# Attention logits from three products instead of four, in a decoder layer on one core

## The chip, the core and the metric

The kernel runs on one NeuronCore of a Trainium2 chip. TensorE multiplies matrices into PSUM (the program uses eight banks of 128 x 512 float32), VectorE and ScalarE work on SBUF and PSUM, GpSimd and SyncE mostly issue transfers. The metric is the device time of one execution in microseconds; lower is better. The kernel before took 1721.38 us, the median of three runs (1719.90 to 1727.16).

## The reference: what is computed

One decoder layer over 1024 tokens of width 1024 in float32: a recurrent branch (RWKV-7, 8 heads of 64) and an attention branch run side by side, are merged by gates, and a SwiGLU feed-forward follows. The change is in the attention branch. An indexer picks at most 256 keys for each query; here that choice is already a bias, 0 for a chosen key and a large negative number for the others. What is left, per head and block of 128 queries:

```python
qb, k, v = rope(q)[block], rope(k), v              # heads of 64
logits = einsum('bqhd,bqkhd->bqhk', qb, kg).astype(float32) * Dh ** -0.5
logits = where(valid, logits, -inf)
prob = softmax(logits, axis=-1)
out = einsum('bqhk,bqkhd->bqhd', prob, vg)
```

## The kernel before, in words

Products that need float32 accuracy are made from two reduced-precision parts of each operand, hi = x rounded and lo = x - hi. The dense layers add three products, hi x hi, hi x lo and lo x hi (`mm3`: line 142 and line 143 alternate over the contraction, line 147 follows). The attention logits of a head contract over only 64 numbers, so hi and lo of the query are stacked to 128 rows, and the key's part stands in both halves: the first product gives (q_hi + q_lo) k_hi, the second (q_hi + q_lo) k_lo. That is two products of 128 rows for each head and each piece of up to 512 keys (line 1081).

The 1024 tokens are worked in two halves of 512. `attend(half)` goes over 4 pairs of heads and, in each, over 4 blocks of 128 queries: 16 units. Block b looks at (b + 1) x 128 keys, 128 to 512 in the first half (one piece) and 640 to 1024 in the second (two pieces). A unit has these steps:

- logits (line 1081) into PSUM tiles called `mix`; line 1083 on VectorE adds the bias, moves the tile to SBUF as `L` and keeps the running maximum; line 1086 on ScalarE takes the exponential and its sum;
- turn (line 1095): TensorE transposes the exponentials in 128 x 128 tiles, ScalarE copies them to SBUF as `pt` (line 1097);
- values (line 1105): transposed probabilities times values, in plain float32, 64 columns a head, so that the two heads of a pair write the two halves of PSUM's rows; the sums of a pair of heads stay in one `mix` bank for four units;
- close: the sums of the exponentials are inverted and multiplied in.

The steps are staggered: with the logits of unit i go the transposes of unit i - 1 and the values of unit i - 2. There are five `mix` banks, shared with the recurrent branch, and three `acc` banks for the dense layers.

TensorE's order is the order in which the code is written. Dense work is a generator in a list named `fill`; `pump(n)` takes steps from it worth n products. In the first half the attention itself is in that list, two of its steps for two steps of the gate products (`blend`), and the recurrent branch (`rwkv`, with the 64-row products of line 573, the row sums of line 603 and the transposes of line 720) pumps the list. In the second half `attend` is the outer loop: each `yield n` pumps n products of the feed-forward layer of the first half. The other engines' order is set by a scheduler when the program is built.

Keys, queries and values come from DRAM, where `proj_qk` has put them (`rope_b` stores each rotated tile on SyncE's queue, line 352). `load` and `load_q` bring those of the next pair of heads on GpSimd's queue two units ahead. Weights arrive on SyncE's queue, or on ScalarE's in part of the program, in three staging buffers (`wst`), and lines 116 and 117 split them into hi (ScalarE) and lo (VectorE).

## Time and profile before

| what | value |
|---|---|
| median of three runs | 1721.38 us |
| the profiled execution | 1716.4 us, its span 1714.6 us |
| TensorE busy, share of the span | 1686.0 us, 98% |
| VectorE, ScalarE, GpSimd busy | 1191.1, 892.7, 104.2 us |
| HBM traffic over the span | 192.92 MB read, 53.00 MB written |
| first half's attention | from about 514 to 668 us |
| second half's attention | from about 976 to 1137 us |

TensorE's busy time is a union of lengths that are modelled: a product of 512 columns has a length of 0.39 us, but the next one starts 0.23 us after it. So the starts in the timeline tell what a product costs, and the busy share only whether TensorE stood still. A row of the timeline is a run of like instructions: start in us, length, engine, line, operation, output and inputs, rows x columns of the array, the shape of the moving operand, and how many.

### The profile page before, as it was taken

The page shows a single profiled execution, that of the slowest core. Times are in us where ns is not written, and L with a number is a line of the kernel's source. Part 1 is how long each engine was busy: PE and PEld are TensorE (multiplying, and loading weights), DVE is VectorE, ACT ScalarE, POOL GpSimd, SP SyncE. Part 2 cuts the span into 40 slices and gives each one's busy share as a digit, 9 for nine tenths or more (in the row PEclk, how much of TensorE's full clock was granted, in tenths as well). Part 3 has the DMA queues.
Part 4 walks back from the last instruction along what each step waited for, and adds up shares of the span by engine and source line. Part 5 has one row for each costly group of instructions (what it writes and reads, how often), then busy time and mean ns, then how long its engine had stood idle before and what let it go on. Part 6 is the DMA issues. An engine that isn't in the chain of part 4 may idle for free.

```text
span 1714.6 us, 28086 instructions
## 1 busy us (share of the span) xinstructions
PE 1686.0 (98%) x10684; PEld 1421.2 (83%) x10684; DVE 1191.1 (69%) x2314; ACT 892.7 (52%) x1720; POOL 104.2 (6%) x127
## 2 busy tenths in 40 slices
PE   8999999999999998999999999999999999999998
PEld 6888888878778777878787888888888799899998
DVE  6789889966568567957886555535474886686764
ACT  6365998453555688755334355533333544353442
POOL 0000000000021111000100211000000000000002
PEclk9999999999999999999999999999999999999999
DMA  5542334446357535653343865254455344624532
GB/s 214 173 141 91 97 109 148 146 111 173 99 179 208 161 104 172 198 161 119 94 135 98 234 160 150 62 184 148 165 175 175 111 148 136 183 90 147 170 111 99
DMA packets 143287, 247.77 MB, mean 145 GB/s; under 512 B 49152, under 2 KB 71360, under 8 KB 143024
## 3 DMA queue, kind: packets, MB, share of 16 engines
q1 hardware_dynamic: 119072, 170.76, 32.4%
q10 hardware_dynamic: 16128, 48.60, 9.1%
q0 software_dynamic: 7952, 26.61, 5.8%
q8 instruction: 84, 1.38, 0.3%
q14 instruction: 51, 0.42, 0.1%
HBM read 192.92 MB, written 53.00 MB: 143 GB/s over the span
## 4 chain that ended last, share of the span: by engine, by line
PE 89%; DVE 4%; ACT 3%; DMA 2%; issue 1%; POOL 1%; ACTq 0%; POOLq 0%; DVEq 0%; SPq 0%
PE acc L142 19%; PE acc L143 19%; PE acc L147 19%; PE acc L160 4%; PE mix L1487 2%; PE mix L1490 2%; PE mix L1488 2%; PE mix L1105 2%; PE mix L1081 2%; PE mix L1095 2%; PE mix L946 2%; DMA wst<-in_w_ffn_in 1%; PE mix L142 1%; PE mix L143 1%; PE mix L147 1%
## 5 line engine op out<-in xcount | busy, mean ns | idle before, releaser
L117 DVE TENSOR_TENSOR wlo<-wst,whi 128x1024 fp32r<-128x1024 f32 (+1 forms) x204 | 249.5, 1224 | 179.2 <-PE acc L147 79.8
L116 ACT ACTIVATE whi<-wst 128x1024 fp32r<-128x1024 f32 (+1 forms) x204 | 213.4, 1047 | 187.3 <-PE acc L143 131.7
L142 PE MATMUL acc<-zhi,whi 128*128 128x512 f32 x416 | 165.7, 398 | 0.7 <-ACT zhi L116 0.7
L143 PE MATMUL acc<-zlo,whi 128*128 128x512 f32 x416 | 162.9, 392 | 1.2 <-DVE zlo L117 1.2
L142 PE MATMUL acc<-u1hi,whi 128*128 128x512 f32 x320 | 127.9, 400 | 0.0
L143 PE MATMUL acc<-u1lo,whi 128*128 128x512 f32 x320 | 125.0, 391 | 0.0
L142 PE MATMUL acc<-u0hi,whi 128*128 128x512 f32 (+1 forms) x320 | 122.8, 386 | 0.0
L143 PE MATMUL acc<-u0lo,whi 128*128 128x512 f32 (+1 forms) x320 | 121.3, 382 | 0.0
L147 PE MATMUL acc<-zhi,wlo 128*128 128x512 f32 x416 | 107.5, 394 | 0.0
L142 PEld LDWEIGHTS acc<-zhi,whi 128*128 128x128 f32 x416 | 78.4, 188 | 18.1 <-issue 1.7
L142 PE MATMUL acc<-fhi,whi 128*128 128x512 f32 x234 | 92.0, 393 | 0.1
L143 PEld LDWEIGHTS acc<-zlo,whi 128*128 128x128 f32 x416 | 78.5, 189 | 16.3 <-DVE zlo L117 1.5
L143 PE MATMUL acc<-flo,whi 128*128 128x512 f32 x234 | 91.2, 390 | 0.0
L147 PEld LDWEIGHTS acc<-zhi,wlo 128*128 128x128 f32 x416 | 76.9, 189 | 15.6 <-issue 0.7
L147 PE MATMUL acc<-u1hi,wlo 128*128 128x512 f32 x320 | 81.8, 395 | 0.0
L147 PE MATMUL acc<-u0hi,wlo 128*128 128x512 f32 (+1 forms) x320 | 78.6, 384 | 0.0
L1086 ACT ACTIVATE L<-L,mx 128x128 f32<-128x128 f32 (+7 forms) x64 | 49.6, 775 | 48.0 <-DVE mx L1083 47.6
L996 ACT ACTIVATE junkl<-kept,z 128x1024 int8<-128x1024 int16 (+1 forms) x64 | 69.4, 1085 | 4.7 <-DVE kept L965 4.4
L142 PEld LDWEIGHTS acc<-u1hi,whi 128*128 128x128 f32 x320 | 60.1, 188 | 12.6 <-issue 0.9
L142 PEld LDWEIGHTS acc<-u0hi,whi 128*128 128x128 f32 x320 | 60.2, 188 | 11.9 <-issue 0.4
L143 PEld LDWEIGHTS acc<-u1lo,whi 128*128 128x128 f32 x320 | 60.1, 188 | 11.3
L147 PEld LDWEIGHTS acc<-u1hi,wlo 128*128 128x128 f32 x320 | 58.9, 188 | 12.5 <-issue 0.9
(438 smaller groups left out, 4036.3 us busy)
## 6 DMA issues: line engine op xcount, KB each, us to landing
wst<-in_w_ffn_in SPq DMA_DIRECT2D x72, 512.0 KB, 3.9
wst<-in_w_in ACTq DMA_DIRECT2D x36, 512.0 KB, 4.4
wst<-in_w_in SPq DMA_DIRECT2D x27, 512.0 KB, 3.9
wst<-in_w_fo SPq DMA_DIRECT2D x25, 512.0 KB, 3.6
k<-d_k POOLq DMA_DIRECT2D x24, 512.0 KB, 7.7
h<-in_xT SPq DMA_DIRECT2D x32, 256.0 KB, 5.2
d_g<-tmp ACTq DMA_DIRECT2D x32, 256.0 KB, 3.5
tmp<-d_g SPq DMA_DIRECT2D x32, 256.0 KB, 3.3
```

The costliest lines, as they stand in the source:

```text
L116: A.activation(hi, x, AF.Copy)
L117: V.tensor_tensor(lo, x, hi.bitcast(F32), op=ALU.subtract)
L142: T.matmul(ps, whi[:, wk + k, :], ahi[:, ak + k, tok], start=k == 0, stop=False)
L143: T.matmul(ps, whi[:, wk + k, :], alo[:, ak + k, tok], start=False, stop=False)
L147: T.matmul(ps, wlo[:, wk + k, :], ahi[:, ak + k, tok], start=False, stop=k == nk - 1)
L160: T.matmul(ps, w[:, k, :], a[:, k, tok], start=k == 0 and j == 0, stop=k == nk - 1 and j == 2)
L946: T.matmul(ps[:, :w], iq[:, h, :], ik[:, i, c:c + w], start=i == 0, stop=i == 1)
L996: A.activation(junka[:, :n], y, AF.Sign, bias=z[:, i:i + 1], accum_out=cnt[:, i:i + 1])
L1081: T.matmul(ps[:, :w], q[bi // 2][:, e, bi % 2 * 128:bi % 2 * 128 + 128], k[:, i, e, c:c + w], start=i == 0, stop=i == 1)
L1086: A.activation(L[:, :n], L[:, :n], AF.Exp, scale=-1.0, bias=last, accum_out=sm[:, bi, e:e + 1])
L1095: T.transpose(ps[:, j * 128:(j + 1) * 128], L[:, (c + j) * 128:(c + j + 1) * 128], ident)
L1105: T.matmul(py[64 * e:64 * e + 64, bi * 128:(bi + 1) * 128], v[:, j, 64 * e:64 * e + 64], pts[e][j // 4][:, j % 4, :], start=j == b, stop=j ...
```

## The change

The keys of a pair of heads are loaded as one 128-row tile per head instead of two: head 0 has hi in the upper 64 rows and lo in the lower ones, head 1 the other way round. The first product (line 1076 of the new kernel, 128 rows) has q_hi in both halves and gives q_hi (k_hi + k_lo). The second (line 1079, 64 rows) gives q_lo k_hi, head 0 in the upper row half of the array and head 1 in the lower one. The product of the two lo parts is no longer made. The logits of both heads of a unit are made in one go, first all 128-row products, then all 64-row products with the heads alternating, and the values of unit i - 2 follow at once. Then come the pumps and the transposes of unit i - 1. The DRAM layout of the keys has head and part swapped, and each rotated key tile is stored in four transfers instead of two.

```diff
@@ -498,8 +498,8 @@
 
         for g, bank in enumerate((acc, mix)):
             yield from proj_rope(CT_AK + 2 * g, us, pj, cs, lambda half: [
-                (slice(64 * a, 64 * a + 64), d_k[half][2 * g + a].rearrange("(i e) p t -> i e p t", i=2))
-                for a in range(2)], acc=bank)
+                (slice(32 * a, 32 * a + 32), d_k[half][2 * g + a // 2].rearrange("(e i) p t -> i e p t", i=2)
+                 [:, a % 2:a % 2 + 1]) for a in range(4)], acc=bank)
             yield from proj_rope(CT_Q + 2 * g, us, pj, cs, lambda half: [
                 (slice(0, 128), d_q[half][:, 4 * g:4 * g + 4])], scale=0.125, acc=bank)
 
@@ -1045,46 +1045,46 @@
         blocks, nk = blocks_of[half], (half + 1) * HT
 
         def load(hp, behind=None):
-            eng = G
-            k = p.tile([128, 2, 2, nk], F32R, tag="k", name="k", bufs=2)
+            k = p.tile([128, 2, nk], F32R, tag="k", name="k", bufs=2)
             if behind is not None:
                 for h in range(half + 1):
-                    G.tensor_copy(k[:, 0, 0, h * HT:h * HT + 2], behind)
+                    G.tensor_copy(k[:, 0, h * HT:h * HT + 2], behind)
             for h in range(half + 1):
-                for e in range(2):
-                    eng.dma_start(k[64 * e:64 * e + 64, :, :, h * HT:(h + 1) * HT].rearrange("p i g t -> p (i g) t")
-                                  .bitcast(F32), d_k[h][hp].rearrange("c p t -> p c t"))
+                for x, planes in enumerate((slice(0, 4, 3), slice(1, 3))):
+                    G.dma_start(k[64 * x:64 * x + 64, :, h * HT:(h + 1) * HT].bitcast(F32),
+                                d_k[h][hp][planes].rearrange("e p t -> p e t"))
             v = p.tile([128, nk // 128, 128], F32, tag="v", name="v", bufs=2)
             for h in range(half + 1):
-                eng.dma_start(v[:, 4 * h:4 * h + 4, :],
-                              d_v[h][:, :, hp * 128:(hp + 1) * 128].rearrange("t p c -> p t c"))
-            return k, [], v
-
-        def load_q(hp, part):
-
-            q = p.tile([128, 2, 256], F32R, tag="q", name="q", bufs=2 + 2 * half)
-            for i in range(2):
-                G.dma_start(q[64 * i:64 * i + 64, :, :].bitcast(F32),
-                            d_q[half][i, 2 * hp:2 * hp + 2, :, part * 256:part * 256 + 256].rearrange("g p t -> p g t"))
-            kqv[hp][1].append(q)
-
-        def logits(hp, bi, e, kqv, sm):
-            k, q, v = kqv
+                G.dma_start(v[:, 4 * h:4 * h + 4, :],
+                            d_v[h][:, :, hp * 128:(hp + 1) * 128].rearrange("t p c -> p t c"))
+            qh = p.tile([128, 2, HT], F32R, tag="qh", name="qh", bufs=2)
+            ql = p.tile([128, HT], F32R, tag="ql", name="ql", bufs=2)
+            for x in range(2):
+                G.dma_start(qh[64 * x:64 * x + 64].bitcast(F32),
+                            d_q[half][0, 2 * hp:2 * hp + 2].rearrange("e p t -> p e t"))
+            G.dma_start(ql.bitcast(F32), d_q[half][1, 2 * hp:2 * hp + 2].rearrange("e p t -> (e p) t"))
+            return k, qh, ql, v
+
+        def logits(bi, kqv, sm):
+            k, qh, ql, v = kqv
             b = blocks[bi]
-            n = (b + 1) * 128
-            L = p.tile([128, nk], F32, tag="L", name="L", bufs=4)
-            mx = smp.tile([128, 2], F32, tag="mx", name="mx", bufs=4)
-            last = -NEG
-            for ci, (c, w) in enumerate(pieces(n)):
-                ps = mix()
-                for i in range(2):
-                    T.matmul(ps[:, :w], q[bi // 2][:, e, bi % 2 * 128:bi % 2 * 128 + 128], k[:, i, e, c:c + w],
-                             start=i == 0, stop=i == 1)
-                V.tensor_tensor_reduce(L[:, c:c + w], ps[:, :w], bias[b][:, c:c + w], -1.0, last,
+            n, toks = (b + 1) * 128, slice(bi * 128, bi * 128 + 128)
+            Ls = [p.tile([128, nk], F32, tag="L", name="L", bufs=4) for _ in range(2)]
+            mxs = [smp.tile([128, 2], F32, tag="mx", name="mx", bufs=4) for _ in range(2)]
+            parts = [(ci, slice(c, c + w), e, mix()[:, :w]) for ci, (c, w) in enumerate(pieces(n)) for e in range(2)]
+            for ci, cols, e, ps in parts:
+                T.matmul(ps, qh[:, e, toks], k[:, e, cols], start=True, stop=False)
+            for ci, cols, e, ps in parts:
+                r = slice(64 * e, 64 * e + 64)
+                T.matmul(ps, ql[r, toks], k[r, e, cols], start=False, stop=True)
+            for ci, cols, e, ps in parts:
+                L, mx = Ls[e], mxs[e]
+                V.tensor_tensor_reduce(L[:, cols], ps, bias[b][:, cols], -1.0, mx[:, ci - 1:ci] if ci else -NEG,
                                        ALU.add, ALU.min, mx[:, ci:ci + 1])
-                last = mx[:, ci:ci + 1]
-            A.activation(L[:, :n], L[:, :n], AF.Exp, scale=-1.0, bias=last, accum_out=sm[:, bi, e:e + 1])
-            return L
+                if cols.stop == n:
+                    A.activation(L[:, :n], L[:, :n], AF.Exp, scale=-1.0, bias=mx[:, ci:ci + 1],
+                                 accum_out=sm[:, bi, e:e + 1])
+            return Ls
 
         def turn(bi, L):
             b, pts = blocks[bi], []
@@ -1099,7 +1099,7 @@
             return pts
 
         def values(bi, pts, kqv, py):
-            b, v = blocks[bi], kqv[2]
+            b, v = blocks[bi], kqv[3]
             for j in range(b, -1, -1):
                 for e in range(2):
                     T.matmul(py[64 * e:64 * e + 64, bi * 128:(bi + 1) * 128], v[:, j, 64 * e:64 * e + 64],
@@ -1159,22 +1159,11 @@
                 hp, bi = units[i]
                 if i == 0:
                     kqv[hp] = load(hp)
-                    load_q(hp, 0)
-                    load_q(hp, 1)
                 if bi == 2 and hp < 3:
                     kqv[hp + 1] = load(hp + 1, sms[hp][:, 0, :] if half else None)
-                    load_q(hp + 1, 0)
-                    load_q(hp + 1, 1)
                 if bi == 0:
                     sms[hp] = smp.tile([128, 4, 2], F32, tag="sm", name="sm", bufs=3)
-                Ls[i] = []
-            for e in range(2):
-                if i < len(units):
-                    Ls[i].append(logits(hp, bi, e, kqv[hp], sms[hp]))
-                    yield 5 if half else (bi + 3) // 2
-                if 0 <= i - 1 < len(units):
-                    ptss.setdefault(i - 1, []).append(turn(units[i - 1][1], Ls[i - 1][e]))
-                    yield 4 if half else (units[i - 1][1] + 3) // 2
+                Ls[i] = logits(bi, kqv[hp], sms[hp])
             if i >= 2:
                 hp2, bi2 = units[i - 2]
                 if bi2 == 0:
@@ -1182,11 +1171,19 @@
                 values(bi2, ptss.pop(i - 2), kqv[hp2], pys[hp2])
                 if bi2 == 3:
                     ri = close1(sms[hp2])
-                yield 4 if half else bi2 + 1
+            yield 9 if half else (bi + 2 if i < len(units) else 0) + (bi2 + 1 if i >= 2 else 0)
+            if i >= 2:
                 if bi2 == 3:
                     closing.append((2, hp2, ri))
                 elif closing:
                     close(closing)
+            if 0 <= i - 1 < len(units):
+                ptss[i - 1] = []
+                for e in range(2):
+                    ptss[i - 1].append(turn(units[i - 1][1], Ls[i - 1][e]))
+                    yield (5, 7)[e] if half else (units[i - 1][1] + 3) // 2
+                    if half and e == 0 and i >= 2 and bi2 == 3:
+                        close(closing)
         while closing:
             yield -6
             close(closing)
```

Two places of TensorE's order and one of ScalarE's, as the programs are built. `L` and `pt` are the exponentials and their transposes, `k`, `q`, `qh`, `ql` keys and queries, `v` the values, `zhi`, `zlo`, `u1hi`, `u1lo` operands of the dense filler. First, the second half, the third pair of heads where its largest block (512-column logits) begins, before:

```order
L1081 MATMUL mix<-k,q 128x448 x4
L147 MATMUL acc<-zhi,wlo 128x512 x4
L1095 MATMUL mix<-kc,L 128x128 x6
L147 MATMUL acc<-zhi,wlo 128x512 x4
L1105 MATMUL mix<-pt,v 64x128 x10
L142 MATMUL acc<-zhi,whi 128x512
L143 MATMUL acc<-zlo,whi 128x512
L142 MATMUL acc<-zhi,whi 128x512
L143 MATMUL acc<-zlo,whi 128x512
L1125 MATMUL mix<-kc,ri 8x128
L1081 MATMUL mix<-k,q 128x512 x4
```

and now:

```order
L143 MATMUL acc<-zlo,whi 128x512
L1076 MATMUL mix<-k,qh 128x512 x4
L1079 MATMUL mix<-k,ql 128x512 x4
L1105 MATMUL mix<-pt,v 64x128 x12
L142 MATMUL acc<-zhi,whi 128x512
```

Before, one head's logits had dense products behind them and the values stood among dense products; now the logits of both heads, the 64-row products and the values are one run.

Second, the first half, before:

```order
L1095 MATMUL mix<-kc,L 128x128 x3
L1081 MATMUL mix<-k,q 128x512 x2
L147 MATMUL acc<-u1hi,wlo 128x512 x8
L1095 MATMUL mix<-kc,L 128x128 x3
L1105 MATMUL mix<-pt,v 64x128 x4
L142 MATMUL acc<-u1hi,whi 128x512
```

and now:

```order
L1095 MATMUL mix<-kc,L 128x128 x2
L1076 MATMUL mix<-k,qh 128x512 x2
L1079 MATMUL mix<-k,ql 128x512 x2
L1105 MATMUL mix<-pt,v 64x128 x4
L147 MATMUL acc<-u1hi,wlo 128x512 x8
```

Here a head's pair of products became two products for both heads and two 64-row ones.

ScalarE's order around the exponentials of a 1024-key block (line 1086, now 1085) in the second half, before:

```order
L1086 ACTIVATE L,sm<-L,mx 128x1024
L1097 ACTIVATE pt<-mix 128x384
L1086 ACTIVATE L,sm<-L,mx 128x1024
L1097 ACTIVATE pt<-mix 128x512
L1097 ACTIVATE pt<-mix 128x384
```

and now:

```order
L1085 ACTIVATE L,sm<-L,mx 128x1024 x2
L1097 ACTIVATE pt<-mix 128x512
L1097 ACTIVATE pt<-mix 128x384
L1097 ACTIVATE pt<-mix 128x512
L116 ACTIVATE fhi<-tmp 128x512
L1097 ACTIVATE pt<-mix 128x384
```

Both heads' exponentials now stand ahead of all copies of the unit before.

## The prediction

> **What bounds the kernel now.** I read the page's totals and its chain first, then TensorE's timeline where the attention stands, then the waits of TensorE, and last the VectorE and ScalarE rows that the attention's products wait for.
>
> ```profile
> span 1714.6 us, 28086 instructions
> PE 1686.0 (98%) x10684; PEld 1421.2 (83%) x10684; DVE 1191.1 (69%) x2314; ACT 892.7 (52%) x1720; POOL 104.2 (6%) x127
> PE 89%; DVE 4%; ACT 3%; DMA 2%; issue 1%; POOL 1%; ACTq 0%; POOLq 0%; DVEq 0%; SPq 0%
> ```
>
> TensorE is busy for 98% of the span and makes 89% of the chain. Its program order is written out in the code, so what counts is the distance from the start of one product to the start of the next. That distance I call a slot. The two stretches that hold the attention, first half (514 to 668 us) and second half (976 to 1137 us), are no exception:
>
> ```profile
> 514.00:668.00 154.00, 150.38 (x1332) 119.17 (x1330) 105.76 (x266) 108.25 (x267) 19.98 (x23) 1.00 0.53 156
> 976.00:1137.00 161.00, 160.76 (x1125) 133.77 (x1124) 84.41 (x190) 87.80 (x166) 16.23 (x30) 1.00 0.46 127
> ```
>
> In the second half TensorE lacks 0.2 us of 161, so a slot taken out there is time won, and a slot or a wait put in is time lost. In the first half it lacks 3.6 us of 154.
>
> **Removed: a quarter of the logits' products.** Per head and piece of keys there are now two products over 128 rows; afterwards there is one such product, and a 64-row product that shares the array with the other head's. The slots, from the timeline (start in us, modelled length, line, count):
>
> ```profile
> 1087.66 0.75 PE L1081 MATMUL mix<-k,q 128*128 128x320 f32 x4
> 1088.25 0.39 PE L142 MATMUL acc<-zhi,whi 128*128 128x512 f32 x1
> ...
> 1057.82 0.86 PE L1081 MATMUL mix<-k,q 128*128 128x384 f32 x4
> 1058.51 0.39 PE L142 MATMUL acc<-zhi,whi 128*128 128x512 f32 x1
> ...
> 1067.95 0.97 PE L1081 MATMUL mix<-k,q 128*128 128x448 f32 x4
> 1068.77 0.40 PE L142 MATMUL acc<-zhi,whi 128*128 128x512 f32 x1
> ...
> 1002.08 1.08 PE L1081 MATMUL mix<-k,q 128*128 128x512 f32 x4
> 1003.00 0.40 PE L142 MATMUL acc<-zhi,whi 128*128 128x512 f32 x1
> ...
> 545.00 0.34 PE L1081 MATMUL mix<-k,q 128*128 128x128 f32 x2
> 545.17 0.62 PE L1095 MATMUL mix<-kc,L 128*128 128x128 f32 x4
> 545.55 0.47 PE L142 MATMUL acc<-u1hi,whi 128*128 128x512 f32 x1
> ...
> 553.06 0.48 PE L1081 MATMUL mix<-k,q 128*128 128x256 f32 x2
> 553.38 0.40 PE L142 MATMUL acc<-u1hi,whi 128*128 128x512 f32 x1
> ```
>
> Second half: one head's four products take 0.59, 0.69, 0.82 and 0.92 us for the four blocks of queries (0.148 to 0.23 us each). Both heads have eight products in a block; six slots remain, so two are saved, half of each figure: (0.59 + 0.69 + 0.82 + 0.92) / 2 = 1.51 us per pair of heads, 6.0 us for the four pairs. First half: four products in a block become three slots, so one is saved: 0.085 us at 128 keys, 0.12 to 0.16 at 256, and, by the rows above, 0.17 at 384 and 0.23 at 512. That is about 0.62 us per pair of heads, 2.5 us for four. Together **-8.5 us**, if the two 64-row products really run at once.
>
> **Do they?** No 64-row product of this number type stands in the trace. The nearest are 64-row products in plain float32, on alternating row halves of the array, in the recurrent branch (the rows marked x2 are cut out of the sixteen by a narrow window):
>
> ```profile
> 342.48 0.39 PE L143 MATMUL acc<-u0lo,whi 128*128 128x512 f32 x1
> 342.80 2.00 PE L573 MATMUL mix<-wa,wup 64*128 64x256 f32 x16
> ...
> 343.55 0.38 PE L573 MATMUL mix<-wa,wup 64*128 64x256 f32 x2
> ...
> 343.77 0.38 PE L573 MATMUL mix<-wa,wup 64*128 64x256 f32 x2
> ...
> 344.73 2.14 PE L147 MATMUL acc<-u0hi,wlo 128*128 128x512 f32 x8
> 346.70 0.49 PE L473 MATMUL mix<-kc,tmp 128*128 128x128 f32 x3
> ```
>
> Two instructions of 256 columns start together and the next two 0.22 us later, while a full-height float32 instruction of half as many columns needs 0.095 us (the four transposes from 545.17 to 545.55). So one of 256 columns alone would need about 0.2 us, and the pairs do overlap. I take the pair as one slot. The other bound is two slots for a pair, no saving: 0 us.
>
> The Trainium skill ("TensorE: Matmul & The Clock Gate", measured speedup of packing) gives 3.07 times for four row tiles, not 4, so a packed group would cost 1.3 slots instead of one. By that the 8.5 us that the pairs occupy would become 11.1, an estimate from that page, and the sum below would move by +2.6 us. The row above shows no such surplus beyond its entry and exit.
>
> **Added: changes of the array's shape.** The row above also shows what it costs to go from full height to 64 rows and back. The last full product before it has a slot of 0.32 us where 0.23 is usual: +0.09. Inside, one pair follows the other after 0.22 us (343.77 - 343.55), so eight would take 1.76 us, and take 1.93: +0.17. The eight products behind it take 1.97 us, against eight at 0.23 = 1.84: +0.13. Together 0.39 us a visit. The value products, 64 columns wide, pay nearly the same today:
>
> ```profile
> 1084.83 0.39 PE L147 MATMUL acc<-zhi,wlo 128*128 128x512 f32 x1
> 1085.15 1.53 PE L1105 MATMUL mix<-pt,v 128*64 128x128 f32 x24
> 1086.61 0.50 PE L142 MATMUL acc<-zhi,whi 128*128 128x512 f32 x1
> 1086.95 0.40 PE L143 MATMUL acc<-zlo,whi 128*128 128x512 f32 x1
> ...
> 1094.38 1.75 PE L1105 MATMUL mix<-pt,v 128*64 128x128 f32 x28
> 1096.05 1.20 PE L147 MATMUL acc<-zhi,wlo 128*128 128x512 f32 x4
> ```
>
> Entry 0.32 against 0.23 (+0.09); 24 instructions in 1.46 us, where two pairs more cost 1.67 - 1.46 = 0.21, so 0.105 a pair and 1.26 for twelve (+0.20); the first product behind 0.34 against 0.23 (+0.11): 0.40 us. So each of the two edges costs about 0.2 us. In the new order the 64-row group stands between the full products and the values: three edges where there were two, **+0.2 us**. This happens for 14 of the 16 blocks in each half; the first two blocks have no values behind them and pay a whole visit, 0.40. Sum: 28 x 0.2 + 4 x 0.4 = **+7.2 us**. No row shows an edge straight from 64 rows to 64 columns with work like this around it; the bounds are 0 and a whole visit of 0.4 us, so 1.6 to 12.8 us. I take the middle, since full-to-narrow and narrow-to-full both came out near 0.2.
>
> The Trainium skill ("TensorEngine Tiling (Array Packing)", key properties) says that changing the tiling mode, not just the tile, drains TensorE. It speaks against this change; it has no figure, and the trace's 0.39 and 0.40 us a visit agree with it. What an edge costs it does not say, so the sum goes by the rows.
>
> **Moved: the order of a block.** A block's work was logits of head one, transposes of one head of the block before, logits of head two, transposes, values, with other products between all of them. Now both heads' logits and the values come in one piece, then 9 products, transposes, 5, transposes, 7. Filler per block in the second half goes from 22 to 21 units of one product; what is not placed there is run later, so it costs nothing. In the first half the attention hands over 50 times instead of 80, against the same 80 hand-overs of gate products taken two for two, so it ends earlier and the last gate products run alone. VectorE and ScalarE have the same instructions in a denser stretch. TensorE waits there now for, among others:
>
> ```profile
> PE mix L1081 <- ACT x L581: 0.8, 1, 0.8
> PE mix L1095 <- DVE mx L1083: 0.7, 1, 0.7
> ```
>
> These 1.5 us come of five PSUM banks shared by the recurrence and the attention. Some go (the attention has left when line 581 comes round again), others come. I take 0, with ends -2 and +2.
>
> In the second half all four logits banks of a block are now filled at once, and with the running value bank that is all five. The rows that set when they come free (the first column of each is the start):
>
> ```profile
> 1077.76 0.69 DVE L1083 CUSTOM_DVE_ANT_0 L<-mix,kept 128x512 f32<-128x512 f32 x1 [1.06 <-PE mix L1081]
> 1078.98 0.74 DVE L1083 CUSTOM_DVE_ANT_0 L<-mix,kept,mx 128x512 f32<-128x512 f32 x1
> 1079.63 0.98 ACT L1097 ACTIVATE pt<-mix 128x512 f32<-128x512 f32 x2 [1.55 <-PE mix L1095]
> 1080.49 1.16 ACT L1086 ACTIVATE L<-L,mx 128x1024 f32<-128x1024 f32 x1
> 1081.53 0.20 ACT L1086 ACTIVATION_READ_ACCUMULATOR L<-L,mx 128x1 f32 x1
> 1061.36 1.06 ACT L116 ACTIVATE whi<-wst 128x1024 fp32r<-128x1024 f32 x1
> ```
>
> For the largest block, from the first logits product: four reductions end near 1.3 + 4 x 0.8 = 4.5 us; the second exponential near 6.4 (the first waits for the third reduction, and each takes 1.36); ScalarE then copies head one's transposes (0.98, to 7.4), splits one weight tile (1.06, to 8.5) and copies head two's, which TensorE finishes near 8.5: 9.5. TensorE's own block is 1.6 of logits, 1.7 of values, 21 x 0.23 = 4.8 of filler and 2 x 0.8 of transposes, 9.7 us, and it wants the first of those two banks 0.5 us later. It comes out even, with 0.7 us to spare. I take 0.
>
> Keys and queries: the DMA issue of keys halves, that of queries grows by half. All are on GpSimd's queue and issued two blocks, near 19 us, ahead, so I cost them at nothing; landing takes 7.7 us (first row below), and if that cover were gone one landing would show. The 16 stores of keys become 32 of half the size on SyncE's queue, where each is issued in about 0.6 us, so at most 16 x 0.6 = 9.6 us spread over 60 us in which that queue mostly waits for VectorE. Behind them stand weight loads; a delay of 0.6 us is covered by the three staging buffers.
>
> ```profile
> k<-d_k POOLq DMA_DIRECT2D x24, 512.0 KB, 7.7
> L352 SPq DMA_DIRECT2D d_k<-stg x16: 574/598/907, 259.6 to 319.6; - x16
> ```
>
> **Sum.** -8.5 + 7.2 + 0 = -1.3 us. The profiled execution took 1716.4 us (span 1714.6 and 1.8 around it), so it becomes 1715.1. The median of the runs, 1721.4, stands 5.0 above that execution; I carry this over: **1720 us**.
>
> **Rivals.**
> A. The banks decide, and it gets slower. Place: the third logits product of a second-half block, waiting for ScalarE's last copy of head two's transposes. It decides from 0.7 us of further delay on ScalarE or VectorE, less than one 1.06 us weight split. For it: both engines serve the feed-forward filler too, and their order is fixed. Against it: ScalarE is busy 87.8 of 161 us there. Price: 0.4 to 1 us in each of 16 blocks, 6 to 16 us, so 1726 to 1736; I name 1730.
> B. The pairs don't overlap at one pass a column: 0 saved, 7.2 added, 1728.6. Against it are the rows of line 573, for it only that these are of another number type.
> C. The edge from 64 rows to 64 columns is free, or hides the loads that the other edges show: -8.5 + 1.6 = -6.9, with up to 2 us of waits gone -8.9: 1712.5 to 1714.5.
> D. The order does not do what the code says. The built order shows the third products in one row, followed at once by the values, so I leave this no chance.
>
> **Chances.** Forecast (1716 to 1725) 0.60, A 0.18, B 0.08, C 0.14. This kernel's measurements can tell about 0.5%, 8.6 us, from no change. Beyond it on the fast side lie a third of C with a few of the forecast's tail and denser first half, 0.13; on the slow side half of A, a third of B and a little else, 0.14; 0.73 is within. The range that holds all but two in ten reaches from C's fast end to A's middle and a little further: 1711 to 1731.
>
> **What would show it.** Right: 64-row products starting in pairs, six slots a block; about 0.32 us between the last full logits product and the first pair, and about as much extra at the values; TensorE still without gaps over 0.15 us in the second half. Wrong: waits of line 1076 for ScalarE's copies (A), a pair taking two slots (B), no extra at the values' first pair (C), or a stretch of the first half in which TensorE waits for the recurrence.

## The result, and the profile after

The changed kernel takes 1735.04 us, the median of six runs (1729.06 to 1737.63), against 1722.01 us of the kernel before on the same chip: a ratio of 1.0068, with a 95% interval of 1.0053 to 1.0083. It is slower, by about 13 us; the forecast was 1720.0 us with a range up to 1731. The profiled execution took 1734.9 us.

The first lines of its page:

```profile
span 1733.2 us, 28111 instructions
PE 1692.7 (98%) x10684; PEld 1419.7 (82%) x10684; DVE 1187.7 (69%) x2314; ACT 895.4 (52%) x1720; POOL 101.5 (6%) x119
```

TensorE still shows 98%, so the totals hide the loss. The starts of the same product in both timelines show where it lies (us; the recurrent branch goes round four times, once for each quarter of the tokens):

| first product of | before | after | difference |
|---|---|---|---|
| second round (line 573) | 490.1 | 491.0 | +0.9 |
| second round, line 720 | 525.5 | 526.4 | +0.9 |
| second round, line 769 | 578.8 | 588.2 | +9.4 |
| first merge | 679.3 | 690.8 | +11.5 |
| third round, line 769 | 741.2 | 755.3 | +14.1 |
| fourth round, line 573 | 802.4 | 819.5 | +17.1 |
| last group of line 873 | 932.8 | 957.3 | +24.5 |
| second merge | 1238.6 | 1259.1 | +20.5 |
| end of the span | 1714.6 | 1733.2 | +18.6 |

All of it is lost while the first half's attention runs and in the rounds of the recurrence behind it. (From line 720 to line 769 of the second round TensorE makes 367 products after the change and 323 before, so not all of the 8.5 us between these rows are lost there; the whole stretch up to the merge holds as many products as before.) The stretch that holds the second half's attention, 933 to 1239 us before, is 4.0 us shorter. The windows of these stretches (length, TensorE busy, its loads, VectorE, ScalarE, GpSimd, granted clock, DMA share, GB/s), before:

```profile
490.10:679.30 189.20, 180.47 (x1514) 143.37 (x1513) 136.26 (x322) 131.11 (x312) 29.22 (x33) 0.99 0.55 164
679.30:932.80 253.50, 250.45 (x1906) 203.65 (x1906) 187.78 (x395) 129.86 (x266) 15.89 (x7) 0.99 0.46 137
```

And after; the third row is the second half's attention:

```profile
491.00:690.80 199.80, 183.17 (x1514) 142.50 (x1513) 134.47 (x321) 134.45 (x320) 27.88 (x29) 0.98 0.50 148
690.80:957.30 266.50, 257.56 (x1912) 208.46 (x1912) 187.70 (x397) 128.18 (x258) 17.06 (x7) 0.98 0.46 133
1001.00:1158.00 157.00, 157.00 (x1121) 127.16 (x1120) 79.08 (x186) 86.75 (x164) 14.66 (x28) 1.00 0.38 109
```

From the second round to the merge TensorE makes the same 1514 products in 10.6 us more, and stands still for 16.6 us (199.80 - 183.17) instead of 8.7: 7.9 of the 10.6 us are idle time. From the merge to the end of the recurrence it is idle for 8.9 us instead of 3.1. In the second half it does not stand still at all. TensorE's waits (us in total, times, the longest), before:

```profile
...
PE mix L720 <- DVE MT L705: 2.5, 1, 2.5
...
PE mix L638 <- DVE nr L117: 1.7, 2, 1.1
PE mix L646 <- ACT nrT L640: 1.6, 1, 1.6
...
PE mix L862 <- ACT UV L853: 0.7, 1, 0.7
```

And after:

```profile
...
PE mix L720 <- DVE MT L705: 4.6, 1, 4.6
PE mix L638 <- DVE nr L117: 3.6, 2, 2.5
PE mix L646 <- ACT nrT L640: 3.5, 1, 3.5
PE mix L1105 <- ACT pt L1097: 2.9, 5, 1.2
PE mix L1095 <- DVE mx L1082: 2.6, 2, 2.0
PE mix L862 <- ACT UV L853: 2.3, 1, 2.3
```

One of these is new: line 1105 (values) waits for line 1097, which copies the transposes. The wait of line 1095 (transposes) for line 1082, the reduction that empties a logits bank, was there before with 0.7 us. The other four are old waits of the recurrence that grew. A longer wait is not always a loss of that size: the wait of line 720 grew by 2.1 us, but from the last group of line 603 in front of it to the first merge it is 13.9 us instead of 12.9.

**The values' wait**, in the timeline of the first half after the change:

```profile
534.46 0.38 PE L1095 MATMUL mix<-kc,L 128*128 128x128 f32 x2
534.59 0.71 PE L1076 MATMUL mix<-k,qh 128*128 128x512 f32 x2
534.66 1.06 ACT L116 ACTIVATE whi<-wst 128x1024 fp32r<-128x1024 f32 x1 [0.58 <-PE acc L143]
535.23 0.50 PE L1079 MATMUL mix<-k,ql 64*128 64x512 f32 x2
535.62 0.64 ACT L1097 ACTIVATE pt<-mix 128x256 f32<-128x256 f32 x2
536.04 0.93 PE L1105 MATMUL mix<-pt,v 128*64 128x128 f32 x8 [0.31 <-ACT pt L1097]
```

The loop ends with the transposes of block i - 1; its next turn begins with the logits of block i + 1, and the values of block i - 1 follow at once. So a block's values stand right behind its own transposes, with the logits of one block and a few filler products between. Here there is no filler between the transposes at 534.46 and the values at 536.04, and ScalarE splits a weight tile (1.06 us) before it copies. Before the change the next block's transposes and their filler lay between as well.

**The bank's wait** and what follows it:

```profile
574.91 1.04 PE L1120 MATMUL mix<-kc,ri 128*64 128x128 f32 x16
577.34 0.51 DVE L1082 CUSTOM_DVE_ANT_0 L<-mix,bias 128x384 f32<-128x384 f32 x1
577.92 0.69 PE L1095 MATMUL mix<-kc,L 128*128 128x128 f32 x2 [1.96 <-DVE mx L1082]
578.83 0.63 PE L143 MATMUL acc<-u1lo,whi 128*128 128x512 f32 x1
579.26 0.63 PE L142 MATMUL acc<-u1hi,whi 128*128 128x512 f32 x1
```

All five `mix` banks are in use when the transposes want one: the sums of the pair of heads that is being closed, those of the next pair, the closing's own bank (line 1120), and now two with logits, where the kernel before filled one at a time. VectorE comes to the reduction only at 577.34, behind a weight split and the work of the gates and the recurrence. The products behind the 2 us wait then stand 0.43 us apart (579.26 - 578.83) instead of 0.23: half the clock (the window from 578 to 580 us has a granted clock of 0.50). Such a wait can be paid twice.

**The pairs and the edges**, in the second half:

```profile
1126.18 0.40 PE L143 MATMUL acc<-zlo,whi 128*128 128x512 f32 x1
1126.41 0.97 PE L1076 MATMUL mix<-k,qh 128*128 128x448 f32 x4
1127.32 0.67 PE L1079 MATMUL mix<-k,ql 64*128 64x448 f32 x4
1127.92 1.31 PE L1105 MATMUL mix<-pt,v 128*64 128x128 f32 x20
1129.16 2.11 PE L147 MATMUL acc<-zhi,wlo 128*128 128x512 f32 x8
1131.11 1.75 PE L160 MATMUL acc<-fhi,whi 128*128 128x512 f32 x7
```

At 448 columns a slot was 0.82 / 4 = 0.205 us. The four full products take 0.91 us, 0.09 over; the four 64-row products take 0.60, two slots and 0.19; the ten pairs of values take 1.24, 0.19 over ten times 0.105; the eight products behind them 1.95, 0.11 over 1.84. So two 64-row products share one slot, and the visit with its three edges costs 0.58 us.

### The profile page after: what moved, and what is told of

Its sections match the earlier page's. It is cut to its first block, busy times and chain, and to the rows that moved or that the text cites. A ratio compares the mean times of both kernels' runs of the same rounds, so it can differ in the third digit from the quotient of the medians.

```text
span 1733.2 us, 28111 instructions
## 1 busy us (share of the span) xinstructions
PE 1692.7 (98%) x10684; PEld 1419.7 (82%) x10684; DVE 1187.7 (69%) x2314; ACT 895.4 (52%) x1720; POOL 101.5 (6%) x119
## 4 chain that ended last, share of the span: by engine, by line
PE 49%; DVE 1%; ACT 0%; DMA 0%; issue 0%; POOL 0%; POOLq 0%; ACTq 0%; DVEq 0%
PE acc L142 10%; PE acc L147 10%; PE acc L143 10%; PE acc L160 3%; PE mix L1487 2%; PE mix L1485 2%; PE mix L1484 2%; PE mix L1105 1%; PE mix L1095 1%; PE acc L1487 1%; PE acc L1485 1%; PE acc L1484 1%; PE mix L1076 1%; PE mix L1079 1%; PE acc L1386 0%; DMA out_T<-h 0%
## 5 line engine op out<-in xcount | busy, mean ns | idle before, releaser
L143 PEld LDWEIGHTS acc<-u1lo,whi 128*128 128x128 f32 x320 | 60.6, 189 | 11.5
L147 PEld LDWEIGHTS acc<-u1hi,wlo 128*128 128x128 f32 x320 | 58.8, 188 | 13.4 <-issue 1.6
```

The lines of the kernel that those rows point to most:

```text
L143: T.matmul(ps, whi[:, wk + k, :], alo[:, ak + k, tok], start=False, stop=False)
L147: T.matmul(ps, wlo[:, wk + k, :], ahi[:, ak + k, tok], start=False, stop=k == nk - 1)
```

## The experiments

Each expectation was written down before its kernel ran. Times are medians; ratios are to the kernel before, measured beside it. Every kernel computes the whole layer.

### Which half: the old and the new attention, half by half

`attend_old` is `attend` of the kernel before, with both its order and its products, reading the keys from the new layout in DRAM.

```diff
# first half old
-        yield from blend(attend(0, at0[0][1], bias), gates, 2, 2)
+        yield from blend(attend_old(0, at0[0][1], bias), gates, 2, 2)
# second half old
-        for n in attend(1, ap, bias):
+        for n in attend_old(1, ap, bias):
```

> The attention of the first half is written as before (two 128-row products per head and piece, the old order of logits, transposes and values, keys read from the new DRAM layout), that of the second half as changed. Theory W (in the first half the new order puts the values of a block right behind the transposes of the same block, so TensorE waits for ScalarE's copies, and its clock falls behind such waits): the stretch from line 720's second visit to line 769's second visit, 53.3 us before and 61.7 us changed, is back at 53 to 54 us; the second half keeps its 157 us instead of 162; in all 1715 to 1719 us, below the kernel before. Rival S (the losses come from the recurrence's own waits in the third and fourth quarter, lines 638, 646, 720 and 862, which have nothing to do with the attention's order): the stretch still comes back, but 1725 to 1730 us remain.

> The other way round: the first half as changed, the second half as before. W: the whole loss of the first half stays and the gain of the second is missing, 1736 to 1742 us, and the second half's stretch is at 162 us. If the loss sat in the second half or in the key stores, this kernel would be near 1722 us.

| first half | second half | median, us | ratio, 95% interval |
|---|---|---|---|
| old | old | 1722.6 | 1 |
| old | new | 1718.7 | 0.9981 [0.9966, 0.9996] |
| new | old | 1741.5 | 1.0103 [1.0087, 1.0119] |
| new | new | 1735.0 | 1.0068 [1.0053, 1.0083] |

The first row is the kernel before, with its own layout in DRAM; the last is the changed kernel's result from above. The first half's attention costs 15 to 19 us, by ratios or by medians; the second half's gains 3 to 4 (0.7 to 5.9 by the interval of the second row) or, beside the new first half, 6. Both times came out as theory W expected. The one with the old first half and the new second half is the fastest of the four. The window of its second round up to the merge:

```profile
492.00:682.90 190.90, 181.69 (x1513) 144.61 (x1513) 135.09 (x322) 131.37 (x312) 29.70 (x33) 0.98 0.56 162
```

Idle time is back at 9.2 us (before: 8.7), line 720 waits 2.7 us and line 646 1.6, the values don't wait, and the transposes wait 0.7 us for a reduction, as they did before the change. The new DRAM layout, with its 32 smaller stores, is in this kernel too, so it costs nothing that shows.

### The order or the products

The first kernel makes the products of the kernel before in the new order; the second the new products with the values behind the next block's transposes again, in both halves.

```diff
# order only, on the kernel before
+            parts = [(ci, slice(c, c + w), e, mix()[:, :w]) for ci, (c, w) in enumerate(pieces(n)) for e in range(2)]
+            for i in range(2):
+                for ci, cols, e, ps in parts:
+                    T.matmul(ps, q[bi // 2][:, e, bi % 2 * 128:bi % 2 * 128 + 128], k[:, i, e, cols],
+                             start=i == 0, stop=i == 1)
...
# products only, on the changed kernel: the loop over units
                 Ls[i] = logits(bi, kqv[hp], sms[hp])
+                yield 9 if half else bi + 2
+            if 0 <= i - 1 < len(units):
+                ptss[i - 1] = []
+                for e in range(2):
+                    ptss[i - 1].append(turn(units[i - 1][1], Ls[i - 1][e]))
+                    yield (5, 4)[e] if half else (units[i - 1][1] + 3) // 2
             if i >= 2:
...
                 values(bi2, ptss.pop(i - 2), kqv[hp2], pys[hp2])
...
```

> The kernel before with the new order alone: both heads' logits in one go, still with two 128-row products per head and piece, then the values of the block before last, then the transposes; no 64-row product. W: the same waits of the values for the copies as in the changed kernel, the stretch of the first half near 61 us, in all 1730 to 1736 us. Rival P (the loss comes from the 64-row products and the changes of the array's shape in the first half, where the pieces are short): no loss, 1719 to 1724 us.

> The changed kernel with the values put back behind the transposes of the following block, a whole block after their own transposes, so that they no longer stand beside the 64-row products. W: no wait of line 1105 for the copies; each block pays a whole visit of the array to 64 rows (0.40 us) and not one edge (0.2), so the first half costs about 6 - 2.5 = 4 us over the kernel before and the second about 0: 1723 to 1728 us. Rival P: as many changes of shape and more, so no better than the changed kernel, 1735 us or over.

Order only: 1739.9 us, ratio 1.0083 [1.0065, 1.0102]; theory W had expected the loss, but only 1730 to 1736 us. The old products in the new order show the whole loss, with the waits of the changed kernel (here line 1107 is the values and 1097 the transposes):

```profile
PE mix L646 <- ACT nrT L640: 3.5, 1, 3.5
PE mix L1107 <- ACT pt L1099: 3.2, 5, 1.3
PE mix L1097 <- DVE mx L1084: 2.5, 2, 1.8
PE mix L862 <- ACT UV L853: 2.3, 1, 2.3
```

So the loss needs neither the 64-row products nor their edges nor the smaller key tiles. They are not free in the first half: from the second round to the merge this kernel takes 198.2 us and the changed one 199.8.

Products only: 1736.6 us, ratio 1.0074 [1.0058, 1.0091], where 1723 to 1728 were expected. The expectation missed, and this is what it showed. The values' waits are gone, and from line 720 to line 769 of the second round it takes 56.5 us instead of 61.8 (before: 53.3). But the waits of lines 646 and 862 stay at 3.5 and 2.3 us, so these have another cause. In the second half this kernel pays a whole visit of the array for the pairs; what that does is seen below, with the other kernels.

### The account of filler

In the first half an attention block hands over work worth so many products, and `pump` takes these off its account (`credit`). The new `yield`s of the first half add up to 160 products and the old ones to 168. So the account, when the list has run dry in the third round, stands at 0 instead of -5 by a count from the code, and all filler behind it goes about five products further ahead of the recurrence. The traces agree: from the first merge to line 769 of the third round 391 products of the dense layers are made after the change, 387 before it and 387 with the account set back. The first kernel below sets the account back; the second sets three gate steps against two of the attention; the third does both and brings the sum back to 168; the fourth is the products-only kernel with account and sum put right.

```diff
# account: in the third round, where the list has run dry
         run(*fill)
         fill.clear()
+        credit[0] = -5
# three gate steps
-        yield from blend(attend(0, at0[0][1], bias), gates, 2, 2)
+        yield from blend(attend(0, at0[0][1], bias), gates, 2, 3)
# the sum of 168
-            yield 9 if half else (bi + 2 if i < len(units) else 0) + (bi2 + 1 if i >= 2 else 0)
+            yield 9 if half else ((bi + 3) // 2 * 2 if i < len(units) else 0) + (bi2 + 1 if i >= 2 else 0)
```

> The changed kernel with one number set: where the recurrence's third quarter has emptied the list of fillers, the account of owed products is put to -5, as it stands in the kernel before (the changed one comes there with 0, since its first-half attention is worth 8 products less and the list runs dry 3 products early). Theory C (the losses of the third and fourth quarter come of the filler standing 5 products further on, so that weight transfers on ScalarE's queue wait for their buffer ahead of the recurrence's copies): the waits of line 646 fall from 3.5 to 1.6 us and of line 862 from 2.3 to 0.7 us, the time by 4 to 6 us to 1729 to 1731 us. The first half's stretch stays at 61.7. If the later waits come of something else: 1735 us.

> The changed kernel, with three gate steps (not two) between two steps of the first half's attention, so that the attention, which hands over 50 times instead of 80, is spread over the same gate products as before. Theory W2 (the first half's stretch is lost to waits because there is too little filler between a block's transposes, copies and values): the stretch from line 720's second visit to line 769's second falls from 61.7 us to 55 to 57 us, line 1105 hardly waits for the copies; in all 1727 to 1731 us, since the third and fourth quarter's waits remain. If density doesn't matter: 1735 us as the changed kernel.

> Both remedies: three gate steps between two attention steps, the first-half attention's worth in products as before (168 instead of 160), and the account at -5. W2 and C together: stretch 55 to 57 us, lines 646 and 862 waiting as in the kernel before, in all 1718 to 1724 us. If either theory is wrong it stays above 1727.

> The kernel with the new products but the values in their old place (which came to 1736.6 us against 1723 to 1728 expected), now with the attention's worth of 168 products and the account at -5. C says that its excess was that of the third and fourth quarter: 1725 to 1729 us, lines 646 and 862 as in the kernel before. If it stays at 1735, the 64-row visits cost more than the rows said.

The account alone: 1730.7 us, ratio 1.0043 [1.0026, 1.0061], as expected. The wait of line 646 is as before the change, the wait of line 862 for ScalarE is gone, and those of the attention are as after the change. The waits of lines 720 and 638 are not mended (5.6 and 3.6 us):

```profile
PE mix L720 <- DVE MT L705: 5.6, 1, 5.6
PE mix L638 <- DVE nr L117: 3.6, 2, 2.5
PE mix L1105 <- ACT pt L1097: 3.6, 5, 1.2
PE mix L1095 <- DVE mx L1082: 2.5, 2, 1.8
PE mix L646 <- ACT nrT L640: 1.6, 1, 1.6
```

Five products, 1.2 us of work that is done either way, cost about 4 us by where they stand (0.3 to 8, an estimate from the intervals of the two ratios). ScalarE's waits in the changed kernel show how:

```profile
ACT nrT L640 <- DVE wlo L117: 2.1, 1, 2.1
ACT yb L844 <- DVE wlo L117: 1.9, 1, 1.9
```

Lines 640 and 844 do not read `wlo`. In this part of the program the weight loads (line 123) are issued on ScalarE's queue, and a load that has to wait until VectorE's split of an older tile frees its staging buffer holds up the copies behind it (line 853, for which line 862 waits, follows line 844). Neither row is there before the change, with the old first half, or with the account set back.

Three gate steps: 1749.3 us, ratio 1.0164 [1.0136, 1.0192], and with account and sum 1745.5, ratio 1.0138 [1.0112, 1.0163]. Both expectations, 1727 to 1731 and 1718 to 1724, were wrong in sign. The idea was that more products between the attention's steps would cover its copies. But the attention then ends later, in the third round's chain, and there the same wait is longer. The timeline of the first of them:

```profile
668.50 5.02 POOL L633 TENSOR_TENSOR nr<-nr,mhalf 128x16 f32<-128x16 f32 x1 [31.56 <-DVE nr L629]
673.56 0.21 ACT L116 ACTIVATE nr<-nr 128x16 fp32r<-128x16 f32 x1 [4.46 <-POOL nr L633]
673.68 0.58 ACT L1097 ACTIVATE pt<-mix 128x512 f32<-128x512 f32 x1
674.31 1.97 PE L1105 MATMUL mix<-pt,v 128*64 128x128 f32 x14 [5.51 <-ACT pt L1097]
```

A power on GpSimd takes 5.02 us; ScalarE's conversion of its result stands in ScalarE's queue ahead of the copy of the transposes, and TensorE's values wait 5.5 us for that copy. The window around it, with a granted clock of 0.88:

```profile
656.00:703.00 47.00, 33.63 (x243) 26.02 (x240) 31.81 (x58) 33.14 (x76) 5.02 (x1) 0.88 0.36 110
```

TensorE is idle for 13.4 us of these 47.

Products only with the account put right: 1731.6 us, ratio 1.0055 [1.0035, 1.0076], 2.6 above what was expected and 5.0 below the same kernel without it (3.3 by the ratios). In its window from the second round to the merge, 193.7 us, TensorE is idle for 11.7 us instead of 16.6.

With these kernels the second half can be compared at the same account: the stretch from the last group of line 873 to the second merge, by the starts in the timelines, in us.

| second half's attention | account 0 | account -5 |
|---|---|---|
| old | 304.7 (first half new) | 305.8 (before) |
| old products, new order | 304.5 (order only) | |
| new | 301.8 (the change), 301.8 (three gate steps) | 304.0 (first half old), 304.2 (account), 304.4 (all three) |
| new products, values behind the next transposes | 305.7 | 306.9 |

So the new attention is worth 2.9 us at account 0 and 1.4 to 1.8 at -5. Nearly all of it comes of the products: the order alone is worth 0.2, the new products in this order 2.7. With the values away from the pairs the new products cost 1.0 and 1.1 more than the old attention instead: 3.9 and 2.5 to 2.9 us more than beside the pairs, for 14 more edges, which the prediction's price puts at 2.8.

### The first half's order alone, and the weights' queue

The first kernel is the one with the account set back, and in the first half alone the values come behind the next block's transposes. It differs from the account's kernel in that place (and the sum of 168), and from the products-only kernel with the account put right in the second half alone. The second kernel is the changed one with the weight loads left on SyncE's queue.

```diff
# first half
-            if i >= 2:
+            if half and i >= 2:
...
+            if not half and i >= 2:
+                hp2, bi2 = units[i - 2]
...
+                values(bi2, ptss.pop(i - 2), kqv[hp2], pys[hp2])
...
+                yield bi2 + 1
...
+        credit[0] = -5
# weights' queue
-    wq[0] = A
```

> The changed kernel with three edits, all in or right behind the first half: there the values of block i-2 come behind the transposes of block i-1 again (logits, filler, transposes, filler, transposes, filler, values, filler), the first half hands over work worth 168 products instead of 160, and the filler account starts the third quarter at -5, as before. The second half keeps the new order. It differs from the run with the account alone (1730.7 us) only by the first half's order. Theory O (what costs in the first half is that the values stand too close behind their own transposes, so TensorE waits for ScalarE's copies): no wait of the values for copies over 0.5 us, the stretch from line 720's second visit to line 769's takes 55 to 56.5 us instead of 61, and the second half takes 3 us less than in the kernel with the old place in both halves (1731.6 us); 1723 to 1727 us. Theory P (the order costs nothing, only the place of the filler counts): the stretch stays near 61 us and the time at 1729 to 1732.

> The changed kernel with one edit: the weight loads of the recurrent stage stay on SyncE's queue instead of ScalarE's. Theory Q (in the changed kernel two weight loads stand on ScalarE's queue waiting for a staging buffer, and two of the recurrence's copies, lines 640 and 853, wait 1.9 us each behind them): TensorE's wait of line 646 falls from 3.5 to about 1.6 us and that of line 862 from 2.3 to about 0.7; 1731 us (1729.5 to 1733). Rival: the same loads then hold up the recurrence's small transfers on SyncE's queue, or other waits take over; 1734 to 1738.

First half: 1726.2 us, ratio 1.0016 [1.0004, 1.0028], as theory O expected: 4.5 us below the account's kernel (1 to 8, an estimate from the intervals of the two ratios) and 5.4 below the products-only kernel with the account put right, where the second half's stretch explains 3.0 (303.9 us against 306.9). No wait of line 1105 is left, and the stretch from line 720 to line 769 takes 55.6 us where the account's kernel takes 61.0:

```profile
525.60:581.20 55.60, 55.60 (x339) 42.10 (x338) 38.50 (x124) 28.44 (x69) 9.81 (x13) 1.00 0.68 183
```

TensorE is never idle in it; in the account's kernel it is for 4.1 us. (The stretch holds 339 products here, 366 in the account's kernel and 323 before the change, so its length alone is not the loss.) The wait of line 1095 for a reduction is still there with 1.9 us, as in the products-only kernel with the account put right; without the account that kernel has only 0.8. This profile is of the slowest of the kernel's twelve executions (1733.7 us), so what follows in it is no guide: from line 769 to the third round it takes 67.9 us at a granted clock of 0.92, where the same program, in the products-only kernel with the account put right, takes 62.6 at 1.00.

Weights' queue: 1736.5 us, ratio 1.0071 [1.0059, 1.0083]: no faster, where theory Q expected 1731. Its waits:

```profile
PE acc L142 <- DVE tmp L1207: 11.3, 1, 11.3
...
PE mix L573 <- DMA wup<-in_wa_up: 2.3, 1, 2.3
...
PE mix L646 <- ACT nrT L640: 0.3, 1, 0.3
```

The mechanism is as Q said, for the wait of line 646 falls from 3.5 to 0.3 us, and that of line 862 leaves the list. But in the third round VectorE waits for a transfer of the recurrence on SyncE's queue, and the merge's line 1207 stands behind it on VectorE:

```profile
702.88 0.19 DVE L739 TENSOR_TENSOR tw<-W,N 128x31 f32<-128x31 f32 x1 [6.76 <-DMA N<-d_n]
...
707.59 0.68 DVE L1207 SCALAR_TENSOR_TENSOR tmp<-tmp,acc 128x512 f32<-128x512 f32 x1
```

The rival was right about the time, though up to the first merge the edit gained: from the second round on it takes 193.4 us, against 199.8 in the changed kernel.

## Why the prediction was wrong

**The terms it was built on held.** "I take the pair as one slot" was right: 0.60 us for four 64-row products of 448 columns, with their edges. "Each of the two edges costs about 0.2 us", and three edges a visit, were right: 0.58 us. (The Trainium skill, "TensorEngine Tiling (Array Packing)", key properties, says that changing the mode drains TensorE; the trace agrees and adds the figure.) For the second half these terms make -6.0 + 14 x 0.2 + 2 x 0.4 = -2.4 us; the stretch from line 873 to the second merge became 1.4 to 2.9 us shorter at the same account (2.7 by the products alone), and the time of the kernel with the new second half alone fell by 3.9 us (0.7 to 5.9).

**The second half's banks** came out as worked: no idle time in 157 us. Rival A was wrong in its place, B in its premise (the pairs overlap), and C in its premise (the edge is there).

**The step that failed** is "Moved: the order of a block", and in it the sentence on the first half: "I take 0, with ends -2 and +2". The swap of halves puts the loss there, 15 to 19 us, and the kernel with the order alone, 17 us above the kernel before, says that the order makes it. The step looked at the 1.5 us for which TensorE already waited, and took them as the size of what could come. It read the order of the first half and saw that hand-overs fall from 80 to 50, but not what the hand-overs had covered. It did name a first half in which TensorE waits for the recurrence as a sign of being wrong, and gave it no price. Three things took the place of its 0.

1. The values now stand right behind the next logits, and no longer a whole block behind their own transposes; in the first half only a few filler products lie in between. The prediction worked out when the copies end for the second half, where a block has 21 products of filler, and not for the first. Moving the values back there, with the sum of 168 put right in the same edit, gives back 4.5 us net, although by the prediction's own price it adds 14 x 0.2 = 2.8 us for edges.
2. Rival A's mechanism happened in the first half: two logits banks filled at once bring the count to five while a pair of heads is closed, so the transposes wait for the reduction (2.6 us instead of 0.7), and half-clock products follow. The prediction counted the banks in the second half alone. No kernel takes this wait out by itself, and with gathered logits it comes to 0.8 us in one kernel and 1.9 to 2.6 in the others named here, so what it costs in all is not shown.
3. The attention's `yield`s are worth eight products less in the first half. The prediction counted such a change for the second half and said that what is not placed there is run later, "so it costs nothing". In the recurrence it cost about 4 us; weight loads on ScalarE's queue fell in front of two copies of the chain.

**The median** was carried over from the profiled execution with 5.0 us. The changed kernel's profiled execution lies 0.1 below its median: that one execution of the kernel before was merely a quick one. The miss does not come from this: the sum forecast 1.3 us less, and the time rose by 13.

**What stays open.** With account and order put right the kernel is still 7.5 us above the one with the old first half (6.0 by the two ratios). The prediction's prices give part of it: a whole visit in each block of the first half, 16 x 0.4 = 6.4 us, against 2.5 saved, makes +3.9. The products-only kernel with the account put right has the same program as this one up to the second half, and its profile is of a quick execution. Against the one with the old first half it loses 2.8 us between the second round and the first merge (193.7 against 190.9) and 2.6 from there to the last group of line 873 (256.8 against 254.2). The rest was not taken apart. Of the 13.0 us lost between the first merge and the end of the recurrence, 5.9 are idle time. The account's kernel gives back 7.1 of them, but its second half's stretch is 2.4 us longer. The others were not found in single rows.

## What to carry to other kernels

When both heads' work is gathered into one piece, write down for each hand-over between engines what stood between producer and consumer before and what does now, for the stretch with the least cover, not for the one with the most. Where filler is metered by an account, keep its sum, because a shift of a few products can move transfers in front of other work in the same queue. Where a change helps in one stage and hurts in another, take it in the one: the old first half with the new second half takes 0.9981 [0.9966, 0.9996] of the time before.

## What the runs showed of the hardware

Half the clock can come after a wait of only 2 us: the row at 577.92 waits 1.96 us, and the starts behind it are 0.43 us apart. It need not: in the same execution the row at 667.52 (line 638) waits 2.46 us, and the eight products from 667.65 on take 1.94 us, 0.24 each, at a granted clock of 1.00. The Trainium skill ("TensorE: Matmul & The Clock Gate", Part 1, the HAM clock gate) puts the fall at about 3.4 us of idle time, in windows that run free; here less was enough in the first case and not in the second. Executions of one kernel differ in this, too: those of the kernel with the first half's order alone run from 1722.5 us (mean granted clock 0.996) to 1733.7 (0.990).

A load that waits for its buffer on ScalarE's queue held up unrelated copies by 2.1 and 1.9 us, and a power of 16 columns on GpSimd took 5.02 us (2.9 to 5.2 in the kernel before), behind which ScalarE stood for 4.46.
